# A decoder layer on one core: first loads and casts in halves, the last block of columns summed in two banks, stores from three queues

## The chip, the cores and the metric

The kernel runs on one core of one Trainium2 chip. A core has a matrix engine (PE, TensorE), a vector engine (DVE), a scalar engine (ACT), a small general engine (POOL, GpSimd) and an engine that here only starts transfers (SP). Each runs its own list of instructions strictly in order; they meet through semaphores. Transfers (DMA) are started from a queue of SP, ACT or POOL. The metric is the device time of one execution in microseconds (us), as a median over runs.

## What is computed

One layer of a hybrid decoder over 256 tokens of width 2048, all in float32. Two groups of heads share an input projection; a gated MLP follows, and a last normalisation. Cut to what matters here:

```
h    = rms_norm(x, attn_norm_g)
proj = h @ w_in                          # 2048 -> 4448 columns
y    = concat(rwkv7_mixer(...), mla_mixer(...))      # recurrent heads, attention heads
x    = x + y @ w_out
h    = rms_norm(x, ffn_norm_g)
x    = x + (silu(causal_conv3(h @ w_gate) + conv_b) * (h @ w_up)) @ w_down     # D_FF = 5632
return rms_norm(x, final_norm_g)
```

The reference works in float32. The kernel gets that accuracy from TensorE by splitting each operand in a rounded part "hi" and a rest "lo" and adding three products: hi·hi, hi·lo and lo·hi.

## The kernel before

**Weight pieces.** All weights stream once, in pieces of 128 x 1024 floats (512 KB). `piece()` (lines 125 to 135) starts the load on SP's queue (L127), lets ACT round the whole piece to hi (the cast of L133), and lets DVE form lo = raw − hi (L134). There are three buffers each for raw, hi and lo, so a load waits until the lo of the piece three before it is done.

**The input.** `xsplit(g)` (lines 137 to 146) loads four of the 16 row blocks of the transposed input (L139, one load of 512 KB). ACT scales each block by the norm's gain and rounds it (L143, four instructions of 256 columns). DVE forms the rest (L144). The gain lies in a small tensor `vec`, which ACT's own queue loads first (L122).

**The start.** The loop at lines 328 to 342 goes over g = 0 to 3: it loads input g, for even g also two weight pieces, one for each of two 128-row tiles of the projection, and multiplies (`prod_c`: for four row blocks first the eight products with hi, L175, then the four with lo, L178). SP's order there is the order of the code. The other engines' orders come from a scheduler that works when the program is built. After the loop come the sums of squares of x (`xt`), more tiles of the projection, and `rope_tables()`. In the last, DVE reduces angles (the `rp` tiles, L264 to L290), ACT takes sines (L292), and POOL copies the results to 32 blocks (`sinR`, `cosR`, L300 to L304). POOL also makes the shifted copies of `h` that the recurrent heads need (L383), behind those 32 blocks in its order.

**The MLP.** It goes in two blocks of 24 and 20 tiles of 256 columns of D_FF. Each block ends with the down projection: for each of four groups c of 512 output columns, `prod_a` (lines 188 to 197) accumulates both token blocks (tb 0 and 1, 128 tokens each) in one PSUM bank each, with three matmuls of 512 columns per row block of weights (L195, L196, L197). In the second block, at c = 3, the last four pieces of weights are already held in SBUF (the `wt` tiles). For these, token block 0 is summed to its end first, then token block 1, so that block 0 is finished while PE works on block 1.

**The end.** When a token block of c = 3 is summed, DVE adds it to the residual (L1008), ACT squares it and sums the squares of each token (L1013), and `final(tb)` runs: eight small DVE instructions for the reciprocal root (L216 to L225), the scaling of the four column groups (DVE L954 for c = 3 and L956 for c = 1, ACT L958 for c = 0 and 2), and four stores of 256 KB, all from SP's queue (L959). In the names of the profile the residual's tiles are all `x`.

Of the kernel before, what the change touches and what calls it, by code (L numbers as in the profile page):

```python
# [54 lines left out]
def hybrid_layer(ctx: ExitStack, tc: tile.TileContext, a: dict, out: bass.AP):  # L55
# [16 lines left out]
    def s4(dt=F32, n="s4"):  # L72
        return sb.tile([P, 1024], dt, tag="s4", name=nm(n), bufs=NS4)
# [20 lines left out]
    def mm(n="mm"):  # L94
        return ps.tile([P, 512], F32, tag="mm", name=nm(n), bufs=NMM)
# [38 lines left out]
        last_lo[0] = V.tensor_tensor(lo, raw, hi.bitcast(F32), ALU.subtract).ins  # L134
        return hi, lo

    def xsplit(g):
        raw = s4(n="xraw").rearrange("p (k t) -> p k t", k=4)
        nc.sync.dma_start(raw, xT[:, g * 4:(g + 1) * 4, :])  # L139
        for j in range(4):  # L140
            k = g * 4 + j
            h = xs_[g][:, j, 0, :]
            S.activation(h, raw[:, j, :], AF.Copy, scale=vv("ag", k))  # L143
            last_x[0] = V.scalar_tensor_tensor(xs_[g][:, j, 1, :], raw[:, j, :], vv("ag", k),  # L144
                                               h.bitcast(F32), ALU.mult, ALU.subtract).ins
        return raw
# [41 lines left out]
    def prod_a(accs, pieces, act_hi, act_lo, kt0, n, first, last, tbs=(0, 1)):  # L188
        hi, lo = pieces
        for j in range(n):  # L190
            wh, wl = hi[:, j * 512:(j + 1) * 512], lo[:, j * 512:(j + 1) * 512]
            for tb in tbs:
                ah = act_hi(kt0 + j)[:, tb * P:(tb + 1) * P]
                al = act_lo(kt0 + j)[:, tb * P:(tb + 1) * P]
                PE.matmul(accs[tb], ah, wh, start=first and j == 0, stop=False)  # L195
                PE.matmul(accs[tb], ah, wl, start=False, stop=False)  # L196
                PE.matmul(accs[tb], al, wh, start=False, stop=last and j == n - 1)  # L197
# [129 lines left out]

    with tc.manual_schedule(engines={mybir.EngineType.SP}):
        for g in range(4):
            xsplit(g)  # L330
            if g == 0:
                nc.scalar.dma_start(cst, a["cst"])
            if g % 2 == 0:
                for i in range(2):
                    pcs[i, g // 2] = piece(a["win"][wt0[i], g // 2])
            for i in range(2):
                hl = tuple(u[:, (g % 2) * 512:(g % 2 + 1) * 512] for u in pcs[i, g // 2])
                prod_c(acc0[i], hl, x_hl, g * 4, 4, g == 0, g == 3)
        for h in range(2):
            prod_c(acc0[2], piece(a["win"][26, h]), x_hl, h * 8, 8, h == 0, h == 1)  # L340
        sums(0)
        kacc[0] = in_tile(1)
        dve0 = last_lo[0]
        sums(1)
        kacc[1] = in_tile(2, ch)
        rope_tables()
        lora = s4(n="lora")
        nc.sync.dma_start(lora, a["lora"])
# [598 lines left out]
    def final(tb):  # L947
        part = st("part", 1)
        V.tensor_reduce(part, ssn[:, tb * 4:tb * 4 + 3], AX.X, ALU.add)
        rs3 = rsqrt(ssn[:, tb * 4 + 3:tb * 4 + 4], 1.0 / DM, EPS, 1, V, part)  # L950
        for c in (3, 0, 1, 2):
            xc = x1[c][:, tb, :]
            if c == 3:
                V.scalar_tensor_tensor(xc, xc, rs3, fgb[1][:, 512:1024], ALU.mult, ALU.mult)  # L954
            elif c == 1:
                V.tensor_scalar(xc, xc, rs3, None, ALU.mult)  # L956
            else:
                S.activation(xc, xc, AF.Copy, scale=rs3)  # L958
            nc.sync.dma_start(out[tb * P:(tb + 1) * P, c * 512:(c + 1) * 512], xc)  # L959

    f0 = 0
    for blk, nf in enumerate((24, 20)):
        hh = [s4(F32R, "hh").rearrange("p (k t) -> p k t", k=4) for _ in range(nf // 4)]
        hl = [s4(F32R, "hl").rearrange("p (k t) -> p k t", k=4) for _ in range(nf // 4)]
        for fi in range(nf):
            f = f0 + fi
            accs = []
            for gu in range(2):
                acc = mm()
                for h in range(2):  # L970
                    prod_b(acc, piece(a["wgu"][f, gu, h]), z_hl, h * 8, 8, h == 0, h == 1)
# [24 lines left out]
        for c in range(4):  # L996
            accs = [mm() for _ in range(2)]
            for i in range(n - (4 if blk == 1 and c == 3 else 0)):
                prod_a(accs, piece(a["wdn"][c, f0 // 2 + i]), h_hi, h_lo, i * 2, 2, i == 0, i == n - 1)
                if blk == 1 and i == 2:  # L1000
                    q = n - 4 + c
                    held.append((q, piece(a["wdn"][3, f0 // 2 + q], a8("wt"))))
            for tb in range(2):
                if blk == 1 and c == 3:
                    for i, pc in held:
                        prod_a(accs, pc, h_hi, h_lo, i * 2, 2, False, i == n - 1, (tb,))
                xc = x1[c][:, tb, :]
                V.tensor_tensor(xc, xc, accs[tb], ALU.add)  # L1008
                if blk == 0:
                    continue  # L1010
                o = tb * 4 + c
                scr = sb.tile([P, 512], F32, tag="xs", name=nm("scr"), bufs=2)
                S.activation(scr, xc, AF.Square, accum_out=ssn[:, o:o + 1])  # L1013
                if c < 3:
                    V.tensor_tensor(xc, xc, fgb[c // 2][:, (c % 2) * 512:(c % 2 + 1) * 512], ALU.mult)
                else:
                    final(tb)
        f0 += nf
# [81 lines left out]
```

## Time and profile before

| | us |
|---|---|
| median of 3 runs | 1210.38 (1208.66 to 1212.13) |
| the profiled execution | 1211.12 |
| its span on the core, first to last instruction | 1209.3 |
| PE busy in it | 1166.8 |
| DVE / ACT / POOL busy in it | 819.8 / 583.2 / 82.1 |
| mean granted TensorE clock | 0.985 of full speed |

The span is 1.8 us shorter than the execution's own time, which also counts what lies before and after it. Times inside the profile count from the start of the span. PE is busy through nearly all of it; what PE does not fill lies mostly in the first 50 us, in the recurrent and attention part between 250 and 420 us, and in the last 10 us.

### The profile page before, as it was taken

The numbers are of one execution on the slowest core, as the hardware profiler recorded it, in microseconds if no ns is written. First come the engines' busy times: TensorE is split into PE (matmuls) and PEld (weight loads), VectorE is DVE, ScalarE is ACT, GpSimd is POOL, SyncE is SP. The second block draws the span as 40 slices with busy tenths as digits, with TensorE's granted clock in tenths as the row PEclk, the third lists the DMA queues.
The fourth block names the chain that finished last, engine by engine and source line by source line (L and its number), as shares of the span: only waits on it lengthen the run. The fifth ranks groups of instructions, "written<-read, shape, count | busy, mean of one in ns | idle before, by whom it ended". The sixth has DMA issues, their size and how long they took to land.

```text
span 1209.3 us, 19618 instructions
## 1 busy us (share of the span) xinstructions
PE 1166.8 (96%) x7633; PEld 1029.2 (85%) x7633; DVE 819.8 (68%) x1304; ACT 583.2 (48%) x883; POOL 82.1 (7%) x248
## 2 busy tenths in 40 slices
PE   7899989988798999999999999999999999999996
PEld 7899989987686888888888888888888888888885
DVE  6797659766777556777777776444577777775563
ACT  6674335432334445655555554333455555554442
POOL 1500430301101001000000000000000000000000
PEclk9999999988899999999999999999999999999998
DMA  8555454734142555555555555556655555566672
GB/s 325 164 159 158 147 167 156 209 108 144 54 157 85 170 187 184 183 188 192 190 192 190 191 191 191 191 191 191 205 194 187 192 192 190 192 219 209 209 211 85
DMA packets 61486, 215.90 MB, mean 179 GB/s; under 512 B 7376, under 2 KB 8144, under 8 KB 61392
## 3 DMA queue, kind: packets, MB, share of 16 engines
q1 hardware_dynamic: 58544, 209.22, 52.8%
q0 software_dynamic: 2080, 3.38, 1.3%
q10 hardware_dynamic: 768, 2.05, 0.5%
q8 instruction: 60, 0.98, 0.3%
q14 instruction: 34, 0.28, 0.1%
HBM read 210.48 MB, written 3.41 MB: 177 GB/s over the span
## 4 chain that ended last, share of the span: by engine, by line
PE 87%; DVE 5%; POOL 2%; DMA 2%; ACT 2%; issue 1%; SPq 0%; ACTq 0%; DVEq 0%; POOLq 0%
PE mm L163 27%; PE mm L166 13%; PE mm L195 9%; PE mm L196 9%; PE mm L197 9%; PE mm L175 9%; PE mm L178 4%; PE pg L536 1%; DVE lo L134 1%; DMA T<-dU 1%; ACT hi L133 1%; DMA xraw<-in_xT 1%; PE py L687 1%; PE px L687 1%; POOL sinR L304 0%
## 5 line engine op out<-in xcount | busy, mean ns | idle before, releaser
L134 DVE TENSOR_TENSOR lo<-raw,hi 128x1024 fp32r<-128x1024 f32 x376 | 460.2, 1224 | 287.6 <-ACT hi L133 281.3
L133 ACT CAST hi<-raw 128x1024 fp32r<-128x1024 f32 x376 | 394.9, 1050 | 490.6 <-issue 223.6
L163 PE MATMUL mm<-z,hi 128*128 128x512 f32 x1408 | 351.3, 392 | 0.0
L163 PEld LDWEIGHTS mm<-z,hi 128*128 128x128 f32 x1408 | 251.9, 188 | 43.7
L166 PEld LDWEIGHTS mm<-z,lo 128*128 128x128 f32 x1408 | 188.3, 188 | 14.5
L166 PE MATMUL mm<-z,lo 128*128 128x256 f32 x1408 | 191.6, 278 | 0.0
L175 PE MATMUL mm<-x,hi 128*128 128x256 f32 x1056 | 147.8, 289 | 14.5 <-ACT hi L133 8.1
L175 PEld LDWEIGHTS mm<-x,hi 128*128 128x128 f32 x1056 | 135.4, 195 | 17.1 <-ACT hi L133 8.1
L196 PE MATMUL mm<-lo,hh 128*128 128x512 f32 x336 | 130.7, 389 | 0.0
L197 PE MATMUL mm<-hi,hl 128*128 128x512 f32 x336 | 130.7, 389 | 0.0
L195 PE MATMUL mm<-hi,hh 128*128 128x512 f32 x336 | 119.7, 389 | 0.0
L178 PE MATMUL mm<-x,lo 128*128 128x256 f32 x528 | 77.4, 286 | 0.0
L197 PEld LDWEIGHTS mm<-hi,hl 128*128 128x128 f32 x336 | 63.1, 188 | 13.2
L195 PEld LDWEIGHTS mm<-hi,hh 128*128 128x128 f32 x336 | 63.1, 188 | 13.0
L196 PEld LDWEIGHTS mm<-lo,hh 128*128 128x128 f32 x336 | 63.1, 188 | 13.0
L178 PEld LDWEIGHTS mm<-x,lo 128*128 128x128 f32 x528 | 69.6, 193 | 0.2
L196 PE MATMUL mm<-lo,yhi 128*128 128x512 f32 x128 | 51.5, 403 | 0.0
L197 PE MATMUL mm<-hi,ylo 128*128 128x512 f32 x128 | 50.5, 394 | 0.0
L195 PE MATMUL mm<-hi,yhi 128*128 128x512 f32 x128 | 49.7, 406 | 0.0
L974 POOL MEMSET gt<- 128x2 f32 x44 | 4.3, 99 | 575.9 <-DVE hl L986 559.0
L197 PEld LDWEIGHTS mm<-hi,ylo 128*128 128x128 f32 x128 | 24.2, 189 | 5.1
L196 PEld LDWEIGHTS mm<-lo,yhi 128*128 128x128 f32 x128 | 24.2, 189 | 5.0
(282 smaller groups left out, 1113.1 us busy)
## 6 DMA issues: line engine op xcount, KB each, us to landing
raw<-in_wgu SPq DMA_DIRECT2D x176, 512.0 KB, 3.3
raw<-in_wdn SPq DMA_DIRECT2D x88, 512.0 KB, 4.2
raw<-in_win SPq DMA_DIRECT2D x70, 512.0 KB, 3.6
raw<-in_wout SPq DMA_DIRECT2D x32, 512.0 KB, 3.6
raw<-in_wuq SPq DMA_DIRECT2D x6, 512.0 KB, 4.0
xraw<-in_xT SPq DMA_DIRECT2D x4, 512.0 KB, 6.3
xt<-in_x SPq DMA_DIRECT2D x4, 512.0 KB, 6.8
raw<-in_wuv SPq DMA_DIRECT2D x4, 512.0 KB, 3.8
```

The source lines that it names most:

```text
L133: S.copy(hi, raw)
L134: last_lo[0] = V.tensor_tensor(lo, raw, hi.bitcast(F32), ALU.subtract).ins
L163: PE.matmul(acc, hi[:, j * P:(j + 1) * P], act(kt0 + j), start=first and j == 0, stop=False, skip_group_check=True)
L166: PE.matmul(acc[:, :T], lo[:, j * P:(j + 1) * P], act(kt0 + j)[:, 0, :], start=False, stop=last and j == n - 1, skip_group_check=True)
L175: PE.matmul(acc, hi[:, j * P:(j + 1) * P], act(kt0 + j)[:, s, :], start=first and j == 0 and s == 0, stop=False, skip_group_check=True)
L178: PE.matmul(acc, lo[:, j * P:(j + 1) * P], act(kt0 + j)[:, 0, :], start=False, stop=last and j == n - 1, skip_group_check=True)
L195: PE.matmul(accs[tb], ah, wh, start=first and j == 0, stop=False)
L196: PE.matmul(accs[tb], ah, wl, start=False, stop=False)
L197: PE.matmul(accs[tb], al, wh, start=False, stop=last and j == n - 1)
L536: PE.matmul(pg[h][:, o:o + P], BK[pp][hs, gg, w * 2 + r, :, :], AR[pp][hs, gg, w * 2 + r, :, :], start=o == 0, stop=True, skip_group_check ...
L687: PE.matmul(dst[HS[h], a_ * 64:(a_ + 1) * 64], lhsT, rhs, start=n == 0 and a_ == 0, stop=True, skip_group_check=True)
L974: nc.gpsimd.memset(gt[:, 0:2], 0.0)
```

## The change

It has three parts.

1. `first_halves` replaces the first `xsplit(0)` and the first `piece()`. The first input load and the first weight load are each split in two of 256 KB, and they alternate: input, weights, input, weights. ACT casts the first weight piece in pieces of 256, 256 and 512 columns, with the input blocks in pairs in between; DVE does the same with lo.
2. At c = 3 of the second MLP block, token block 1 is summed in two banks of 256 columns (`mmh`, from the pool `ch`) by `prod_h`, with twice as many matmuls of half the width. With the held pieces one half is summed to its end, then the other. Each half has its own add and its own square; the two sums of squares (`sl`) are added by one more DVE instruction.
3. `final` issues its stores from SP (c = 3 and 0), POOL (c = 1) and ACT (c = 2).

```
-        raw = s4(n="xraw")...
-        nc.sync.dma_start(raw, xT[:, g * 4:(g + 1) * 4, :])
-        for j in range(4):
+    def first_halves(src):
...
+        for q in range(2):
+            cs = slice(q * 512, q * 512 + 512)
+            nc.sync.dma_start(xr[:, q * 2:q * 2 + 2, :], xT[:, q * 2:q * 2 + 2, :])
+            nc.sync.dma_start(raw[:, cs], src[:, cs])
+        for q in range(2):
+            cs = slice(q * 256, q * 256 + 256)
+            S.copy(hi[:, cs], raw[:, cs])
+            V.tensor_tensor(lo[:, cs], raw[:, cs], hi[:, cs].bitcast(F32), ALU.subtract)
+            xsplit(0, xr, (q * 2, q * 2 + 1))
+        S.copy(hi[:, 512:], raw[:, 512:])
+        V.tensor_tensor(lo[:, 512:], raw[:, 512:], hi[:, 512:].bitcast(F32), ALU.subtract)
...
-            nc.sync.dma_start(out[tb * P:(tb + 1) * P, c * 512:(c + 1) * 512], xc)
+            eng = (nc.sync, nc.gpsimd, nc.scalar, nc.sync)[c]
+            eng.dma_start(out[tb * P:(tb + 1) * P, c * 512:(c + 1) * 512], xc)
+    def prod_h(acc, pc, q, h_hi, h_lo, kt0, first, last):
+        for j in range(2):
+            wh, wl = (u[:, j * 512 + q * 256:j * 512 + q * 256 + 256] for u in pc)
+            ah, al = (f(kt0 + j)[:, P:2 * P] for f in (h_hi, h_lo))
+            for k, (l, r) in enumerate(((ah, wh), (ah, wl), (al, wh))):
+                PE.matmul(acc[:, :256], l, r, ...)
...
+                prod_a(accs, pc, h_hi, h_lo, i * 2, 2, i == 0, i == n - 1, (0,) if fine else (0, 1))
+                if fine:
+                    for q in range(2):
+                        prod_h(accs[1][q], pc, q, h_hi, h_lo, i * 2, i == 0, False)
...
+                if fine and tb == 1:
+                    sl = st("sl", 2)
+                    for q in range(2):
+                        cs = slice(q * 256, q * 256 + 256)
+                        for i, pc in held:
+                            prod_h(accs[1][q], pc, q, h_hi, h_lo, i * 2, False, i == n - 1)
+                        V.tensor_tensor(xc[:, cs], xc[:, cs], accs[1][q][:, :256], ALU.add)
+                        S.activation(scr[:, cs], xc[:, cs], AF.Square, accum_out=sl[:, q:q + 1])
+                    V.tensor_tensor(ssn[:, 7:8], sl[:, 0:1], sl[:, 1:2], ALU.add)
+                    final(tb)
```

In the new file the lines move: L139 and L127 of the start become L145 and L146 for the halves and L159 and L127 for the rest, L143 becomes L163, L1008 and L1013 become L1049 and L1051 for the halves, L959 becomes L982.

How it moves instructions is seen at three places. The first is ACT at the start of the program, from its first work after the loads of `vec` and `cst`. Before:

```order
L143 ACTIVATE x_65<-xraw_86,vec 128x256 x4
L133 CAST hi_99<-raw_97 128x1024
L133 CAST hi_105<-raw_103 128x1024
L143 ACTIVATE x_66<-xraw_133,vec 128x256 x4
L143 ACTIVATE x_67<-xraw_167,vec 128x256 x4
```

After, `raw_87` and `hi_88` are the first weight piece, and `raw_109` is the second:

```order
L163 ACTIVATE x_65<-xraw_86,vec 128x256 x2
L149 CAST hi_88<-raw_87 128x256 x2
L163 ACTIVATE x_65<-xraw_86,vec 128x256 x2
L152 CAST hi_88<-raw_87 128x512
L133 CAST hi_111<-raw_109 128x1024
L163 ACTIVATE x_66<-xraw_139,vec 128x256 x4
```

The first cast of weights now stands behind two input blocks instead of four, and the piece's cast is three instructions instead of one.

The second place is DVE at the end of the angle reduction in `rope_tables()`, around the lo of a weight piece and the small constants (`om_mu` to `idb`). Before:

```order
L134 TENSOR_TENSOR lo_347<-raw_344,hi_346 128x1024
L361 TENSOR_SCALAR om_mu<-vec 128x27
L272 SCALAR_TENSOR_TENSOR rp_441<-rp_442,rp_441 128x64
L362 TENSOR_SCALAR nkk<-vec 128x8
...
L375 CAST idb<-cst 128x128
L288 TENSOR_TENSOR rp_441<-rp_441 128x64
L272 SCALAR_TENSOR_TENSOR rp_441<-rp_442,rp_441 128x64
L290 TENSOR_SCALAR rp_441<-rp_441 128x64
```

After:

```order
L134 TENSOR_TENSOR lo_353<-raw_350,hi_352 128x1024
L308 TENSOR_TENSOR rp_447<-rp_447 128x64
L383 TENSOR_SCALAR om_mu<-vec 128x27
L384 TENSOR_SCALAR nkk<-vec 128x8
...
L397 CAST idb<-cst 128x128
L292 SCALAR_TENSOR_TENSOR rp_447<-rp_448,rp_447 128x64
L310 TENSOR_SCALAR rp_447<-rp_447 128x64
```

One step of the angles (L272 before) has moved ahead of that lo, so that three of them follow it instead of four.

The third place is DVE at the end, from the finishing of token block 0 to the sum for token block 1. `x_4835` and `x_4841` are the residual of c = 3, `x_4625` and `x_4631` that of c = 1. Before:

```order
L220 SCALAR_TENSOR_TENSOR rt_11683<-ry_11682,rm_11681 128x1
L225 SCALAR_TENSOR_TENSOR ry_11682<-rt_11683,ry_11682 128x1
L954 SCALAR_TENSOR_TENSOR x_4835<-x_4835,ry_11682,fgb_10950 128x512
L956 TENSOR_SCALAR x_4625<-x_4625,ry_11682 128x512
L1008 TENSOR_TENSOR x_4835<-x_4835,mm_11538 128x512
L216 TENSOR_SCALAR rm_11730<-ssn_5337,part_11728 128x1
```

After:

```order
L240 SCALAR_TENSOR_TENSOR rt_11727<-ry_11726,rm_11725 128x1
L1049 TENSOR_TENSOR x_4841<-x_4841,mmh_11545 128x256
L245 SCALAR_TENSOR_TENSOR ry_11726<-rt_11727,ry_11726 128x1
...
L976 SCALAR_TENSOR_TENSOR x_4841<-x_4841,ry_11726,fgb_10956 128x512
L978 TENSOR_SCALAR x_4631<-x_4631,ry_11726 128x512
L1049 TENSOR_TENSOR x_4841<-x_4841,mmh_11546 128x256
L1052 TENSOR_TENSOR ssn_5343<-sl_11745 128x1
L236 TENSOR_SCALAR rm_11803<-ssn_5343,part_11801 128x1
```

The add of the first half now stands inside token block 0's reciprocal root; the add of the second half and the new sum of the two squares (L1052) stand where the one add stood.

More of the change, by code (lines that the diff above doesn't have):

```diff
@@ L135, in piece, with xsplit @@
         return hi, lo
-    def xsplit(g):
-        raw = s4(n="xraw").rearrange("p (k t) -> p k t", k=4)
-        nc.sync.dma_start(raw, xT[:, g * 4:(g + 1) * 4, :])
-        for j in range(4):
+    def first_halves(src):
+        xr = s4(n="xraw").rearrange("p (k t) -> p k t", k=4)
+        raw = sb.tile([P, 1024], F32, tag="raw", name=nm("raw"), bufs=NRAW)
+        hi = sb.tile([P, 1024], F32R, tag="hi", name=nm("hi"), bufs=NHI)
+        lo = sb.tile([P, 1024], F32R, tag="lo", name=nm("lo"), bufs=NLO)
+        for q in range(2):
[9 more added lines that the diff above has]
+        V.tensor_tensor(lo[:, 512:], raw[:, 512:], hi[:, 512:].bitcast(F32), ALU.subtract)
+        return hi, lo
+    def xsplit(g, raw=None, js=range(4)):
+        if raw is None:
+            raw = s4(n="xraw").rearrange("p (k t) -> p k t", k=4)
+            nc.sync.dma_start(raw, xT[:, g * 4:(g + 1) * 4, :])
+        for j in js:
             k = g * 4 + j
@@ L329, in hybrid_layer @@
         for g in range(4):
-            xsplit(g)
             if g == 0:
+                pcs[0, 0] = first_halves(a["win"][wt0[0], 0])
                 nc.scalar.dma_start(cst, a["cst"])
+            else:
+                xsplit(g)
             if g % 2 == 0:
-                for i in range(2):
+                for i in range(1 if g == 0 else 0, 2):
                     pcs[i, g // 2] = piece(a["win"][wt0[i], g // 2])
@@ L958, in final @@
                 S.activation(xc, xc, AF.Copy, scale=rs3)
-            nc.sync.dma_start(out[tb * P:(tb + 1) * P, c * 512:(c + 1) * 512], xc)
+            eng = (nc.sync, nc.gpsimd, nc.scalar, nc.sync)[c]
[5 more added lines that the diff above has]
+            for k, (l, r) in enumerate(((ah, wh), (ah, wl), (al, wh))):
+                PE.matmul(acc[:, :256], l, r, start=first and j == 0 and k == 0, stop=last and j == 1 and k == 2)
     f0 = 0
@@ L997, in hybrid_layer @@
             accs = [mm() for _ in range(2)]
+            fine = blk == 1 and c == 3
+            if fine:
+                accs[1] = [ch("mmh") for _ in range(2)]
             for i in range(n - (4 if blk == 1 and c == 3 else 0)):
-                prod_a(accs, piece(a["wdn"][c, f0 // 2 + i]), h_hi, h_lo, i * 2, 2, i == 0, i == n - 1)
+                pc = piece(a["wdn"][c, f0 // 2 + i])
+                prod_a(accs, pc, h_hi, h_lo, i * 2, 2, i == 0, i == n - 1, (0,) if fine else (0, 1))
+                if fine:
+                    for q in range(2):
+                        prod_h(accs[1][q], pc, q, h_hi, h_lo, i * 2, i == 0, False)
                 if blk == 1 and i == 2:
@@ L1003, in hybrid_layer @@
             for tb in range(2):
-                if blk == 1 and c == 3:
+                xc = x1[c][:, tb, :]
+                if fine and tb == 1:
[5 more added lines that the diff above has]
+                        V.tensor_tensor(xc[:, cs], xc[:, cs], accs[1][q][:, :256], ALU.add)
+                        scr = sb.tile([P, 512], F32, tag="xs", name=nm("scr"), bufs=2)
+                        S.activation(scr[:, cs], xc[:, cs], AF.Square, accum_out=sl[:, q:q + 1])
+                    V.tensor_tensor(ssn[:, 7:8], sl[:, 0:1], sl[:, 1:2], ALU.add)
+                    final(tb)
+                    continue
+                if fine:
                     for i, pc in held:
                         prod_a(accs, pc, h_hi, h_lo, i * 2, 2, False, i == n - 1, (tb,))
-                xc = x1[c][:, tb, :]
                 V.tensor_tensor(xc, xc, accs[tb], ALU.add)
```

## The prediction, made before the changed kernel had run

> **What bounds the kernel now.** I read the page first, then the timeline of the first 32 us, the chain of waits up to 46 us, the windows of the first 80 us, and last the timeline and the transfers of the final 10 us. The page:
>
> ```profile
> span 1209.3 us, 19618 instructions
> PE 1166.8 (96%) x7633; PEld 1029.2 (85%) x7633; DVE 819.8 (68%) x1304; ACT 583.2 (48%) x883; POOL 82.1 (7%) x248
> PE 87%; DVE 5%; POOL 2%; DMA 2%; ACT 2%; issue 1%; SPq 0%; ACTq 0%; DVEq 0%; POOLq 0%
> ```
>
> PE is busy for 96% of the span and makes up 87% of the chain that ended last. The change leaves PE's arithmetic alone, so all it can win lies in the first microseconds, where PE has no data, and in the last ten, where PE is done. The timeline of the start (start, us, engine, line, operation, in brackets the idle time before and its releaser):
>
> ```profile
> 5.28 1.71 ACT L143 ACTIVATE x<-xraw,vec 128x256 fp32r<-128x256 f32 x4 [2.61 <-DMA vec<-in_vec]
> 7.05 1.04 ACT L133 CAST hi<-raw 128x1024 fp32r<-128x1024 f32 x1
> 8.14 2.08 PE L175 MATMUL mm<-x,hi 128*128 128x256 f32 x8 [8.14 <-ACT hi L133]
> 8.40 1.05 ACT L133 CAST hi<-raw 128x1024 fp32r<-128x1024 f32 x1 [0.31 <-DMA raw<-in_win]
> 9.68 3.31 ACT L143 ACTIVATE x<-xraw,vec 128x256 fp32r<-128x256 f32 x8 [0.23 <-DMA xraw<-in_xT]
> ```
>
> PE starts at 8.14 because the first cast ends then. That cast waits in ACT's order for four input blocks, and these wait for `vec`, which lands at 5.28. The second cast waits for its load until 8.40, the next input blocks for theirs until 9.68. The chain of waits behind that, in order of time:
>
> ```profile
> 2.11 7.55 DMA xraw<-in_xT
> ...
> 15.60 5.41 DMA xt<-in_x
> ...
> 27.46 1.14 DVE lo L134
> ...
> 28.69 0.13 DVE rp L272
> ...
> 30.11 0.21 DVE rp L290
> ...
> 30.68 0.40 POOL sinR L304
> ...
> 45.21 0.23 POOL cosR L300
> ```
>
> PE is not on it. What counts is the transfers, then an lo of DVE, the angles behind it, and 15 us of POOL's copies. The windows of 8 us (busy time and count of PE, PEld, DVE, ACT, POOL; granted clock; share of the DMA engines; GB/s):
>
> ```profile
> 16.00:24.00 8.00, 8.00 (x71) 8.00 (x70) 6.75 (x20) 5.20 (x10) 0.00 (x0) 1.00 0.96 323
> 32.00:40.00 8.00, 6.71 (x58) 6.52 (x56) 6.16 (x13) 3.90 (x4) 7.36 (x13) 1.00 0.81 249
> 40.00:48.00 8.00, 6.24 (x40) 6.04 (x40) 4.66 (x11) 4.10 (x9) 7.06 (x25) 0.79 0.50 147
> 56.00:64.00 8.00, 8.00 (x64) 7.48 (x62) 8.00 (x21) 7.41 (x16) 0.20 (x2) 1.00 0.35 105
> ```
>
> The transfers are full at the start (0.96 in the first of these, 0.81 in the next). From 32 to 48 us PE has idle time and POOL has little; in the last window DVE has none. The longest idle time of PE there, from the timeline, and what held the work behind it:
>
> ```profile
> 41.76 3.17 PE L175 MATMUL mm<-x,hi 128*128 128x256 f32 x16 [3.05 <-DVE h L384]
> 45.88 0.48 DVE L387 SCALAR_TENSOR_TENSOR sh<-h,vec,sh 128x256 f32<-128x256 f32 x1 [3.15 <-POOL h L383]
> ```
>
> DVE waits 3.15 for POOL's copy of `h`, which stands behind `cosR` in POOL's order, and PE waits for DVE. So a lead that PE gains at 8 us is spent again at 32 to 48 us, unless POOL's copies start earlier too. The end:
>
> ```profile
> 1198.28 0.48 DVE L956 TENSOR_SCALAR x<-x,ry 128x512 f32<-128x512 f32 x1
> ...
> 1199.35 0.40 PE L197 MATMUL mm<-wt,hl 128*128 128x512 f32 x1
> 1199.79 0.69 DVE L1008 TENSOR_TENSOR x<-x,mm 128x512 f32<-128x512 f32 x1 [1.03 <-PE mm L197]
> 1200.57 0.63 ACT L1013 ACTIVATE scr<-x 128x512 f32<-128x512 f32 x1 [1.62 <-DVE x L1008]
> 1201.32 0.21 DVE L216 TENSOR_SCALAR rm<-ssn,part 128x1 f32<-128x1 f32 x1 [0.85 <-ACT scr L1013]
> 1201.57 0.15 DVE L217 TENSOR_SCALAR ry<-rm 128x1 int32<-128x1 int32 x1
> 1201.76 0.22 DVE L220 SCALAR_TENSOR_TENSOR rt<-ry,rm 128x1 f32<-128x1 f32 x1
> ...
> 1203.11 1.33 ACT L958 ACTIVATE x<-x,ry 128x512 f32<-128x512 f32 x2 [1.82 <-DVE ry L225]
> ...
> 1203.78 0.48 DVE L956 TENSOR_SCALAR x<-x,ry 128x512 f32<-128x512 f32 x1
> 1203.85 1.79 SPq L959 DMA_DIRECT2D out<-x  x4
> ```
>
> Here every step waits for the one before: 9.55 us from PE's last end (1199.75) to the end of the span. Behind the four issues of SP (1203.85 to 1205.64) come the transfers; their share of the 16 engines in tenths, from 1203.5 to 1209.3 in slices of 0.145 us:
>
> ```profile
> DMA  0000000079899999999999999992000000000000
> ```
>
> **Part 1, the halves.** Added: two loads on SP, two more casts, two more lo on DVE. Removed: nothing. The same bytes are asked for in the same order. ACT still starts at 5.28, since `vec` lands then. Two input blocks take 0.86 (half of 1.71). For a cast of 256 columns the nearest row is ACT's square of 256 columns (a group: busy us, mean ns, idle before):
>
> ```profile
> L778 ACT ACTIVATE csq<-cr 128x256 f32<-128x256 f32 x6 | 2.5, 416 | 1.9 <-DVE cr L773 1.6 <-DVE cl L782 0.3
> ```
>
> At 0.416 the first cast ends at 6.56 and PE can start at about 6.6 instead of 8.14, a lead of 1.5. Two such casts, two more blocks and one cast of 512 (0.63 by the square of 512 above) bring ACT to 8.46, and the second piece is cast at 8.46 instead of 8.40. The next blocks still begin at 9.68, when their load is there. So on ACT, and on DVE behind it, nothing after 9.68 moves: both follow the transfers, and these are full. Only PE has a lead, and in the windows it finds idle time of 1.29 (8.00 − 6.71) and 1.76 (8.00 − 6.24) before 48 us, in which DVE and POOL hold it. What moves POOL is DVE's order: one step of the angles now stands ahead of the lo of 27.46, so that `sinR` can start earlier by 0.13 (row of 28.69). Halves may cost bandwidth, since rows of 2 KB per partition stand where rows of 4 KB stood; the late lo would follow by at most as much. I take **−0.1**. The lower end is −1.5, the lead kept whole; the upper +0.5, a sixth of the 3.2 us that 1 MB takes at the 323 GB/s of the window.
>
> **Part 2, two banks.** Token block 1 has ten pieces of six matmuls at c = 3, six pieces in the common loop and four held: 60 matmuls of 512 columns become 120 of 256. Pace and prices have rows elsewhere in the MLP (three of the chain near 563 us, 8 matmuls of 512 columns and twice 8 of 256; then a group):
>
> ```profile
> 563.19 1.83 PE mm L163 x8
> 565.02 0.94 PE mm L166 x8
> 567.79 0.91 PE mm L166 x8
> L184 DVE TENSOR_TENSOR gt<-mm,gt 128x256 f32<-128x256 f32 x44 | 18.4, 417 | 0.0
> ```
>
> One of 512 takes 1.83/8 = 0.2288, two of 256 take 0.2275 to 0.235, in the mean 0.2313: 60 x 0.0025 = **+0.15**, with ends −0.08 and +0.37. Behind PE's last matmul the add falls from 0.69 to 0.42 (**−0.27**) and the square from 0.63 to 0.42 (**−0.21**). The sum of the two halves is a new small step on DVE; the nearest row is L217 at 0.15, and with the gap to its next it costs 0.19 (1201.57 to the next small one at 1201.76): **+0.19**. The first half's add and square are hidden: PE ends that half 24 matmuls (four pieces of six) x 0.1156 = 2.8 us before its last one. The add stands inside token block 0's reciprocal root and delays it by 0.42; that block's last DVE instruction ended at 1198.76 before, so now at about 1199.2, still ahead of PE's end near 1199.9. If that cover went, the second add would wait, 1 us for 1 us. On ACT the second square stands behind block 0's scaling and its store (0.45 an issue, 1.79/4), which end at about 1199.9 too, ahead of the add's end at 1200.3. Part 2 in sum: −0.14.
>
> **Part 3, three queues.** SP issued its four within those 1.79. Now c = 2 is issued at 1204.44 (1203.11 + 1.33) instead of about 1205.2, and c = 1 at 1204.26 from POOL. But the slices show the engines at 0.9 from 1204.66 to 1207.5: the four stores of 1.05 MB are limited by their own transfer, and the last issue is covered by the data before it. An earlier last issue wins only the thin first slices (0.7, 0.9, 0.8): **−0.1**. Lower end −0.3, the same 2.9 us of data with ten tenths instead of nine. The upper end comes from POOL's own transfers (count, KB each, median us to landing):
>
> ```profile
> out<-x SPq DMA_DIRECT2D x4, 256.0 KB, 2.4
> Lp<-dL POOLq DMA_DIRECT2D x1, 512.0 KB, 3.6
> TT<-dT POOLq DMA_DIRECT2D x4, 128.0 KB, 5.9
> ```
>
> By the 3.6 of `Lp` POOL's store lands at 1204.26 + 3.6 = 1207.86, against 1207.56 for the last of before: +0.3. By the 5.9 of `TT`: 1210.16, +2.6. I take it to land with the others, since `Lp` is twice as large.
>
> On this the Trainium skill ("DMA: Bandwidth & Descriptors", section "Issuing engines are not separate DMA queues") says that transfers from the scalar, sync and gpsimd engines all end up on the same 16 DMA engines and that issuing from several saves only the sequencer's time. The tenths above agree: the engines are at 0.9 with one queue. By that page part 3 wins nothing beyond the issue.
>
> **Sum.** −0.1 + 0.15 − 0.27 − 0.21 + 0.19 − 0.1 = −0.34. The profiled execution took 1211.12, so it would take 1210.8; it lies 0.74 above the median of the runs, 1210.38, so I forecast **1210.0**.
>
> **Rivals.**
> - *The lead is kept.* PE is full from 16 to 32 us (71 matmuls in 8.00 us), so a lead of 1.5 can live that long; if POOL's copies then start earlier too, because DVE finds its lo earlier, it lasts to the end. Two facts speak for it: the raw buffers are freed by DVE's lo, and the first piece's lo is done earlier, so that a later load may be asked for earlier. Against it: the transfers are at 0.96. The first eight matmuls took 2.08, 0.26 each, where later ones take 0.1127 (8.00/71): an early start also has the slow stretch over earlier. Time: 1210.0 − 1.4 = 1208.6. The Trainium skill ("TensorE: Matmul & The Clock Gate", section "What's actually happening") has TensorE at half clock until it has been busy for some 3.4 us; the 0.26 against 0.1127 agrees with that, and by the page the cold stretch starts at 6.6 and is over 1.5 earlier.
> - *POOL's store lands last.* It is decided by the 3.3 us from 1204.26 to 1207.56: if POOL needs longer from the wait to the landing, the end moves 1 for 1. `Lp` gives +0.3 and `TT` +2.6; at a middle of 1.4 the sum is −0.34 + 0.1 + 1.4 = +1.2, or 1211.6, slower than before. The Trainium skill ("Advanced Engine Details and Errata", section "DGE: Hardware vs Software") gives about 1 us to the first byte for a transfer from GpSimd and 0.6 for one from sync or scalar. By that the price is an estimated 0.4, less than what its earlier issue gives back.
> - *The halves of the end come out dearer.* If two matmuls of 256 cost 0.235 and block 0 is late on ACT, part 2 is +0.1 instead of −0.14: 1210.3, as before.
>
> **How the numbers follow.** The forecast has a chance of 0.60 (with the third rival, which ends beside it), the kept lead 0.20, POOL's late store 0.15; 0.05 is left for a rearranged stretch before 80 us that moves more. The lowest sum is −1.5 − 0.08 − 0.27 − 0.21 + 0.19 − 0.3 = −2.2, so 1208.2; the highest +0.5 + 0.37 − 0.29 + 2.6 = +3.2, so 1213.6. The range leaves out the last tenth of each side's rare case: 1207.7 to 1212.4, with 0.5 below the lowest sum for the runs' own scatter. A measurement tells a change from none at about 0.3%, 3.6 us: faster is below 1206.7, slower above 1214.0. Neither the lowest nor the highest sum gets there, so faster keeps 0.10 and slower 0.06, out of the kept lead and the unknown rearrangement, and of POOL's store.
>
> **What would show it.** Part 1: the first matmul at 6.6 and the second group of input blocks still at 9.68; `sinR` at 30.5. If `sinR` starts before 29.5 the kept lead is right. Part 2: from PE's last end to L236 1.28 instead of 1.57 us; and the last matmul 0.15 later relative to the start of c = 3. Part 3: the tenths full to the same place, three queues in them, and POOL's store not the last. The prediction is wrong if PE idles less than before between 30 and 50 us, or if the span ends over 1.8 us behind the last store's data.

## The result, and the profile after

The changed kernel took 1214.57 us in the median of 20 runs (1211.36 to 1221.53); the kernel before took 1210.88 beside it. The ratio is 1.0034, with a 95% interval of 1.0021 to 1.0047: slower by 3.7 us, where 1210.0 was forecast and 1212.4 was the end of the range; it is also above the highest sum of the prediction, 1213.6. A few executions, one of them of 5572 us, were disturbed as a whole and do not enter the ratios, which are not simply the quotients of the medians. The profiled execution took 1212.15, with a span of 1210.4, and is one of the fastest of its kernel, so the trace shows only a part of the 3.7.

The timeline of the start after the change, ACT and PE:

```profile
5.10 0.91 ACT L163 ACTIVATE x<-xraw,vec 128x256 fp32r<-128x256 f32 x2 [2.41 <-DMA vec<-in_vec]
6.05 0.71 ACT L149 CAST hi<-raw 128x256 fp32r<-128x256 f32 x2
6.51 2.85 PE L195 MATMUL mm<-x,hi 128*128 128x256 f32 x8 [6.51 <-ACT hi L149]
7.28 0.91 ACT L163 ACTIVATE x<-xraw,vec 128x256 fp32r<-128x256 f32 x2 [0.51 <-DMA xraw<-in_xT]
9.19 1.05 ACT L133 CAST hi<-raw 128x1024 fp32r<-128x1024 f32 x1 [0.49 <-DMA raw<-in_win]
10.47 3.31 ACT L163 ACTIVATE x<-xraw,vec 128x256 fp32r<-128x256 f32 x8 [0.23 <-DMA xraw<-in_xT]
```

PE starts at 6.51, as forecast (6.6). But the second half of the input is there only at 7.28, the second weight piece at 9.19 instead of 8.40, and the next input blocks at 10.47 instead of 9.68. In this pair of profiles the transfers are 0.8 us later. The windows of 4 to 8 us, first of the kernel before, then of the changed one (share of the DMA engines and GB/s are the last two columns):

```profile
4.00:8.00 4.00, 0.00 (x0) 0.00 (x0) 1.68 (x4) 2.66 (x5) 2.46 (x5) 1.00 1.04 411
```

```profile
4.00:8.00 4.00, 1.38 (x5) 1.09 (x5) 1.79 (x5) 2.34 (x6) 2.40 (x5) 1.00 1.02 368
```

The engines are full in both (1.04 and 1.02), and with halves they move 368 GB/s instead of 411. POOL's first copy and PE's wait for `h` in the timeline after:

```profile
31.33 0.40 POOL L324 TENSOR_SCALAR sinR<-rp 32x64 f32<-32x64 f32 x1 [24.93 <-ACT rp L312]
...
42.48 3.46 PE L195 MATMUL mm<-x,hi 128*128 128x256 f32 x16 [3.45 <-DVE h L406]
```

POOL starts 0.65 later (30.68 before) and PE waits 3.45 instead of 3.05, for work that also comes later. One pair of profiles is not enough here: the section on the first loads compares all of them. The end:

```profile
1196.30 0.28 PE L990 MATMUL mmh<-wt,hl 128*128 128x256 f32 x1
...
1199.13 0.28 PE L990 MATMUL mmh<-wt,hl 128*128 128x256 f32 x1
1199.45 0.42 DVE L1049 TENSOR_TENSOR x<-x,mmh 128x256 f32<-128x256 f32 x1 [0.70 <-PE mmh L990]
1199.90 0.42 ACT L1051 ACTIVATE scr<-x 128x256 f32<-128x256 f32 x1 [0.97 <-DVE x L1049]
...
1200.44 0.16 DVE L1052 TENSOR_TENSOR ssn<-sl 128x1 f32<-128x1 f32 x1 [0.57 <-ACT scr L1051]
1200.64 0.21 DVE L236 TENSOR_SCALAR rm<-ssn,part 128x1 f32<-128x1 f32 x1
...
1203.16 0.81 SPq L982 DMA_DIRECT2D out<-x  x2
1203.78 0.35 ACTq L982 DMA_DIRECT2D out<-x  x1
1203.87 0.54 POOL L982 DMA_DIRECT2D out<-x  x1 [4.18 <-DVE x L978]
```

From PE's last end (1199.41) to L236 it takes 1.23 us instead of 1.57, and the stores are issued within 1.25 us instead of 1.79. Yet from PE's last end to the end of the span it takes 1210.4 − 1199.41 = 10.99 instead of 9.55. The share of the DMA engines in the last 8.0 us, in slices of 0.2 us, of the kernel before and of the changed one:

```profile
DMA  9993000000000000199999999999997000000000
```

```profile
DMA  0000000099999999999888000000000000000000
```

The last byte is moved 1.8 us ahead of the end before and 3.6 us ahead of it now: in those 3.6 us the slices show no transfer. POOL's store does land last of the four, since it is issued last and takes longest (count, KB each, median us from issue to landing; SP's four have 2.3):

```profile
out<-x ACTq DMA_DIRECT2D x2, 256.0 KB, 2.8
out<-x POOLq DMA_DIRECT2D x2, 256.0 KB, 3.5
```

Issued at 1203.87, it lands at about 1207.4, some 3.0 us ahead of the end. What SP waits for behind its last issue, in the changed kernel (us in total, times, longest), where before the wait for the stores was 2.2 and that for PE's queue 0.7:

```profile
SPq L1146 <- DMA out<-x: 3.3, 1, 3.3
SPq L1146 <- PEq L1146: 2.3, 2, 1.8
```

The second wait is put down to PE's queue, but PE had ended at 1199.41. Line 1146 is the last of the program, where the queues of all engines meet. Its instructions in POOL's and SP's queues (count, ns min/median/max, first and last start), first of the changed kernel, then of the one before:

```profile
L1146 POOLq EVENT_SEMAPHORE  x4: 17/17/17, 1209.6 to 1210.3; - x4
L1146 POOLq DRAIN  x3: 46/102/5747, 1203.8 to 1210.1; - x3
L1146 SPq DRAIN  x3: 7/7/7, 1207.9 to 1209.8; - x3
```

```profile
L1096 POOLq DRAIN  x3: 46/102/4452, 1062.4 to 1209.1; - x3
```

A DRAIN is an instruction of the queue itself. The first one of POOL starts with the store, at 1203.8, and lasts 5.75 us. SP reaches its own first DRAIN at 1207.9, some 0.5 us behind the last landing. POOL goes on only at 1209.6, when its DRAIN is over, and 0.8 us later the span ends. Before the change POOL's DRAIN took 4.45 us behind a last instruction of 0.10 us at 1062.39, and no one waited for it.

### The profile page after: what moved, and what is told of

It is laid out like the page before. It is cut to its first block, busy times and chain, and to the rows that moved or that the text cites. A ratio compares the mean times of both kernels' runs of the same rounds, so it can differ in the third digit from the quotient of the medians.

```text
span 1210.4 us, 19750 instructions
## 1 busy us (share of the span) xinstructions
PE 1167.0 (96%) x7693; PEld 1030.2 (85%) x7693; DVE 820.3 (68%) x1308; ACT 584.4 (48%) x887; POOL 84.0 (7%) x250
## 4 chain that ended last, share of the span: by engine, by line
PE 75%; issue 13%; DVE 5%; DMA 2%; POOL 2%; ACT 1%; SPq 0%; POOLq 0%; DVEq 0%; ACTq 0%
PE mm L183 25%; PE mm L186 13%; PE mm L195 9%; PE mm L215 6%; PE mm L216 6%; PE mm L217 6%; PE mm L198 4%; PE pg L558 1%; DVE lo L134 1%; DMA T<-dU 1%; DMA raw<-in_win 1%; DMA xraw<-in_xT 1%; ACT hi L133 1%; PE py L709 1%; POOL sinR L324 0%
## 5 line engine op out<-in xcount | busy, mean ns | idle before, releaser
L216 PE MATMUL mm<-lo,hh 128*128 128x512 f32 x324 | 126.1, 389 | 0.0
L217 PE MATMUL mm<-hi,hl 128*128 128x512 f32 x324 | 126.1, 389 | 0.0
L215 PE MATMUL mm<-hi,hh 128*128 128x512 f32 x324 | 115.7, 389 | 0.0
L216 PEld LDWEIGHTS mm<-lo,hh 128*128 128x128 f32 x324 | 60.8, 188 | 12.3
L216 PE MATMUL mm<-lo,yhi 128*128 128x512 f32 x128 | 52.1, 407 | 0.0
L216 PEld LDWEIGHTS mm<-lo,yhi 128*128 128x128 f32 x128 | 24.5, 192 | 5.1
```

## A measure that does not scatter

Runs of one kernel lie some 2 us to either side of their median. In the profiles what differs lies ahead of the MLP: its first matmul starts between 471.4 and 476.5 us, and from it to the first matmul of the first down projection it takes 266.06 us in all of them. From the first matmul of the first down projection to the end of the span, the profiles of kernels that are alike there agree within 0.2 us. Its first row, before and after:

```profile
739.45 0.39 PE L195 MATMUL mm<-hi,hh 128*128 128x512 f32 x1
```

```profile
738.26 0.39 PE L215 MATMUL mm<-hi,hh 128*128 128x512 f32 x1
```

This stretch takes 1209.3 − 739.45 = 469.85 us before and 1210.4 − 738.26 = 472.14 after: 2.29 of the 3.7 us lie in it. The expectations of the later runs call it the stretch from the "second down projection stage"; it is the first block's. In the table it is cut at PE's last end. "Median" is that of 11 or 12 runs, each with some 30 runs of before beside it.

| kernel | median, before beside it | ratio (95%) | to PE's last end | behind it |
|---|---|---|---|---|
| before | 1210.88 | | 460.30 | 9.55 |
| changed (20 runs) | 1214.57 | 1.0034 (1.0021 to 1.0047) | 461.15 | 10.99 |
| e1_halves | 1211.11, 1210.76 | 1.0006 (0.9994 to 1.0019) | 460.29 | 9.37 |
| e2_banks | 1211.63, 1210.76 | 1.0007 (0.999 to 1.0025) | 461.15 | 9.33 |
| e3_queues | 1212.76, 1210.76 | 1.0018 (1.0006 to 1.003) | 460.30 | 11.22 |
| e4_nopool | 1211.84, 1210.76 | 1.0004 (0.9991 to 1.0016) | 461.15 | 9.11 |
| e5_changed | 1213.89, 1211.06 | 1.0035 (1.0016 to 1.0054) | 461.15 | 10.96 |
| e6_banks_queues | 1212.49, 1211.06 | 1.0012 (0.9997 to 1.0028) | 461.15 | 10.95 |
| e7_pool_first | 1211.45, 1211.06 | 1.0006 (0.9993 to 1.002) | 461.14 | 9.14 |
| e8_banks_nopool | 1211.49, 1211.06 | 1.001 (0.9995 to 1.0026) | 461.15 | 9.23 |
| e9_late_banks | 1211.33, 1210.9 | 1.0 (0.9984 to 1.0015) | 460.45 | 9.16 |
| e10_casts | 1209.71, 1210.9 | 0.9983 (0.9964 to 1.0002) | | |
| e11_loads | 1211.68, 1210.9 | 0.9994 (0.9976 to 1.0012) | 460.30 | 9.37 |
| e12_all_loads | 1212.08, 1210.9 | 1.0006 (0.9992 to 1.002) | 460.30 | 9.43 |
| e13_pool_c3 | 1212.72, 1210.82 | 1.0025 (1.0008 to 1.0042) | 461.15 | 10.57 |
| e14_best | 1210.99, 1210.82 | 1.0006 (0.9992 to 1.0019) | 460.45 | 9.18 |
| e15_whole_loads | 1214.24, 1210.82 | 1.0029 (1.0015 to 1.0043) | 461.15 | 10.94 |

In the profile of e10 PE is only half as fast from about 10 us on (45 matmuls in the 10 us from 10 to 20, where in the kernel before 71 fit in 8 us), so only what lies ahead of that is used.

## The experiments

### Each part alone, and the change without a store from POOL

e1 has `first_halves` alone, e2 the two banks alone, e3 the three queues alone. e4 is the changed kernel with

```
-            eng = (nc.sync, nc.gpsimd, nc.scalar, nc.sync)[c]
+            eng = (nc.sync, nc.sync, nc.scalar, nc.sync)[c]
```

> The kernel before with part 1 alone (halves of the first loads and casts). Theory A, three separate costs: the loads in halves bring the second input load later (9.66 to 10.45 in the two profiles) and POOL's first copy later (30.68 to 31.33), so +0.7 us at 80 us, carried to the end: about 1211.6 against 1210.9. Theory B, the granted clock: the slower time comes from more windows of half clock between 240 and 400 us, whatever part shifts the start; then this part alone gives +2 to +4 us with a mean clock 0.002 to 0.004 lower than before. If neither holds, the time is that of before within 1 us.

> The kernel before with part 2 alone (two banks of 256 columns at the end). Nothing ahead of the last stage changes, so both theories agree on the start and the middle. Theory A: from PE's last end to the first small step of the reciprocal root 1.28 us instead of 1.57, PE +0.15: -0.1 to -0.3 us in all. Theory B: the same time as before and the same clock. A result 1 us or more above before would mean that the two banks cost something that the last profile does not show.

> The kernel before with part 3 alone (stores from SP, POOL and ACT). Theory A: the last data of the stores are written about 0.6 us earlier, but the span ends 3.6 us behind the last data instead of 1.7, since a store from POOL is waited for longer: +1.2 to +1.9 us, about 1212.4, with the mean clock of before. Theory B: the stores change the end by less than 0.5 us, the clock is that of before, and so is the time.

> The changed kernel with POOL's store moved to SP (stores of c = 3, 0, 1 from SP and c = 2 from ACT). Theory A: the 3.6 us between the last data and the end go back to about 1.7 and the time falls by 1.2 to 1.9 us against the changed kernel, to some 1213. Theory B: the time and the clock stay those of the changed kernel, about 1214.6 and 0.983.

The queues alone are slower by 1.0006 to 1.003, and 11.22 us lie behind PE's last end. The changed kernel without POOL's store has 9.11 there and is not to be told from before (1.0004). So theory A holds for POOL's store, with a time below the 1213 that it gave. The rows of e3, its last matmul, POOL's last issue and the DMA share in its last 8.0 us:

```profile
1202.48 0.40 PE L197 MATMUL mm<-wt,hl 128*128 128x512 f32 x1
...
1207.63 0.54 POOL L960 DMA_DIRECT2D out<-x  x1 [4.80 <-DVE x L956]
```

```profile
DMA  0000000069999999999999000000000000000000
```

Again 3.6 us of silence. Theory B fails on it: the price is there without any change at the start. The banks alone show what neither theory expected: PE's stretch is longer by 0.85 us (461.15 against 460.30), in every kernel that has them throughout c = 3, and never in one without. Halves alone gave 1.0006, at most 1.0019, with the mean clock of before (0.985): theory B's 2 to 4 us at a lower clock are not seen, and the 0.7 of A is neither shown nor excluded.

### The change again, parts left out, POOL's store made early

e6 is the changed kernel without `first_halves`, e8 the same without POOL's store. e7 lets POOL store for token block 0 only, 5 us earlier:

```
-            eng = (nc.sync, nc.gpsimd, nc.scalar, nc.sync)[c]
+            eng = (nc.sync, nc.gpsimd if tb == 0 else nc.sync, nc.scalar, nc.sync)[c]
```

> The changed kernel once more, beside the three below on one chip. Theory A (a store from POOL at the very end holds the end of the program by some 1.9 us, the rest of the change costs 1 us or less): 11.0 us from PE's last end to the end of the span, and 2 to 3 us over before, 1213 to 1214. Theory B (the 3.7 us are mostly the start in halves, through PE's wait for h and the clock): the same time, but the next kernel takes most of it away and the third none.

> The changed kernel without part 1 (two banks and three queues alone). Theory A: still 11.0 us from PE's last end to the end, and +1.5 to +2 us over before. Theory B: within 0.7 us of before.

> The changed kernel with POOL storing c = 1 of token block 0 only; block 1's stores go from SP (c = 3, 0, 1) and ACT (c = 2). Theory A, with the cost in the lateness of POOL's last store: 9.1 us from PE's last end to the end, as with no store from POOL at all, and within 1 us of before. A rival to that: POOL's queue costs its 1.9 us at the end of the program however early its store was; then 11.0 us again. Theory B: as the changed kernel.

> The kernel before with the two banks and with c = 2 stored from ACT, all else from SP; no halves at the start. Theory A: 9.1 us behind PE's last end instead of 9.55, so -0.4 us against before, which the runs can hardly tell from no change. Theory B agrees. Against the kernel with halves and the same end (which gave +0.5 us over before) it tells what the halves cost: A expects 0 to 1 us.

The result of the change is repeated (1.0035). With POOL's store for block 0 alone the end is that of a kernel without any (9.14 and 9.11), in the last 8.0 us of e7:

```profile
DMA  9997899500000000069999999999999100000000
```

So it is not a store from POOL's queue as such that costs, but one as late as this. The profile of e7 shows why. POOL's DRAIN is as long as in the changed kernel, 5.79 us, but it starts at 1199.9 with the earlier store and is over at 1205.7, while SP comes to its own only at 1208.6:

```profile
L1146 POOLq DRAIN  x3: 46/102/5786, 1199.9 to 1209.1; - x3
```

Without halves and with POOL's store (e6) the end has its 10.95. Its median lies 1.4 over before, close to the 1.5 to 2 that A expected, but so wide (0.9997 to 1.0028) that the runs alone would not show it; the 10.95 do. e8, which has no halves, came to 1.001, and e4, which differs from it by the halves, to 1.0004: this pair shows no cost of halves.

### Cheaper banks, and the first loads taken apart

e9 keeps 512 columns in the common loop and goes to halves for the four held pieces only, in two further banks; the first bank is added to the residual earlier. It has no store from POOL and no halves at the start. Against the changed kernel:

```
+                    V.tensor_tensor(xc, xc, accs[1], ALU.add)
+                    acch = [ch("mmh") for _ in range(2)]
...
-                            prod_h(accs[1][q], pc, q, h_hi, h_lo, i * 2, False, i == n - 1)
+                            prod_h(acch[q], pc, q, h_hi, h_lo, i * 2, i == held[0][0], i == n - 1)
```

e10 is before with the casts in parts and the loads whole, e11 the reverse. e12 has all ten loads of the start loop in two halves each:

```
+        for q in range(2):
+            nc.sync.dma_start(raw[:, q * 2:q * 2 + 2, :], xT[:, g * 4 + q * 2:g * 4 + q * 2 + 2, :])
```

> The kernel before with a cheaper form of part 2: token block 1 keeps 512 columns in the six pieces of the common loop; only the four held pieces go in halves of 256 to two further banks. c = 2 is stored from ACT, the rest from SP; no halves at the start. Theory A by the traces so far: PE from the first matmul of the second down projection stage on loses 0.85 us with two banks throughout, since all 120 matmuls of 256 columns run at 0.118 to 0.120 each; with 48 of them it loses 0.15 to 0.25, and the 9.1 to 9.2 us behind PE's last end stay: from that first matmul to the end 469.7 against 469.85 before and 472.1 in the changed kernel. In all -0.2 us, no change by the runs. Rival: the 0.85 us come from the change of width and not from the number, then 470.3.

> The kernel before with the first weight piece cast in 256, 256 and 512 columns and the first two loads whole. Theory C (the loads in halves are what delays the second input load): that load lands as before, the group of eight input scalings begins at 9.4 to 9.9, PE begins at 7.5 to 8.1; the same time as before within 0.5 us. Theory D (PE's lead itself is turned into a longer wait for h): 0.5 to 1 us over before.

> The kernel before with the first two loads in alternating halves and the casts whole. Theory C: the group of eight input scalings begins at 10.0 to 10.5 instead of 9.4 to 9.9, PE at about 8.1, and the time is 0.5 to 1 us over before. Theory D: no change beyond the runs' scatter.

> The kernel before with all ten loads of the start loop (four of input, six of weights) in two halves each, in the old order, casts whole. This takes the cost of halved loads five times: Theory C: the last input blocks and POOL's first copy are later by 2 us or more (sinR at 32.5 or later instead of 30.7), and the time is 1 to 3 us over before. Theory D, or no cost of halves at all: sinR within 0.5 us of before, and no change.

e9 came out as expected: 460.45 + 9.16 = 469.61. With 48 narrow matmuls instead of 120 PE's stretch is longer by 0.15 us instead of 0.85. That the sum lies 0.24 below before is not won by the halves: the store from ACT accounts for some 0.17 of it, and four kernels with all stores from SP and 512 columns have between 9.37 and 9.55 behind PE's last end.

The narrow matmuls' pace in the common loop of the changed kernel, from the first to the last of eight:

```profile
1175.26 0.28 PE L990 MATMUL mmh<-hi,hh 128*128 128x256 f32 x1
...
1176.10 0.28 PE L990 MATMUL mmh<-lo,hh 128*128 128x256 f32 x1
```

That is 0.84/7 = 0.120 us each, or 0.240 a pair. Where the 0.85 lie is read from the first matmul of c = 3 and the first of the held pieces, before and after:

```profile
1172.26 0.39 PE L195 MATMUL mm<-hi,hh 128*128 128x512 f32 x1
...
1188.58 0.40 PE L195 MATMUL mm<-wt,hh 128*128 128x512 f32 x1
```

```profile
1171.06 0.39 PE L215 MATMUL mm<-hi,hh 128*128 128x512 f32 x1
...
1187.99 0.40 PE L215 MATMUL mm<-wt,hh 128*128 128x512 f32 x1
```

From 739 us to c = 3 it takes 432.80 us in both. The common loop takes 16.93 us instead of 16.32, the held pieces up to PE's last end 11.42 instead of 11.17: +0.61 and +0.25. In the loop before, a wide matmul took 16.32/72 = 0.2267 us. After, by the start times of all rows, the 72 narrow ones take 8.59 us where 36 wide ones took 8.16, and the 36 wide ones of token block 0 between them take 8.34, or 0.2317 each. So the loop loses 0.42 on the narrow ones and 0.18 on the wide ones beside them. e9 leaves the loop at 16.32. Whether the number of narrow ones costs or the alternation with wide ones is not separated.

e10 and e11 take loads and casts apart, with one profile each. In e10, the casts in parts let PE start at 7.45 and the second group of input blocks begins at 9.50, in time (in e14, which opens in the same way, 7.89 and 9.88):

```profile
7.45 2.15 PE L193 MATMUL mm<-x,hi 128*128 128x256 f32 x8 [7.45 <-ACT hi L147]
...
9.50 1.71 ACT L161 ACTIVATE x<-xraw,vec 128x256 fp32r<-128x256 f32 x4 [0.23 <-DMA xraw<-in_xT]
```

In e11, the loads in halves alone bring that group at 10.21 although `vec` was there early, at 4.45. PE starts later than before, at 8.90:

```profile
4.45 0.91 ACT L159 ACTIVATE x<-xraw,vec 128x256 fp32r<-128x256 f32 x2 [1.77 <-DMA vec<-in_vec]
...
8.90 2.07 PE L191 MATMUL mm<-x,hi 128*128 128x256 f32 x8 [8.90 <-ACT hi L148]
...
10.21 0.91 ACT L159 ACTIVATE x<-xraw,vec 128x256 fp32r<-128x256 f32 x2 [0.24 <-DMA xraw<-in_xT]
```

In place this agrees with theory C, though PE was expected at 8.1. In size C expected too much. e12 has five times the halves; POOL starts at 32.00, between D's bound and C's. The times of e11 (0.9994, up to 1.0012) and e12 (1.0006, up to 1.002) neither show what C expected of them nor exclude it. The window of e12 from 4 to 8 us shows 365 GB/s, where the changed kernel has 368.

All profiles together say less than these pairs. The second group begins between 9.96 and 10.47 in the eight kernels with halves, and with whole first loads between 9.36 and 9.93 in eight and at 10.21 in e15. POOL's first copy starts between 30.39 and 31.33 in the seven kernels with halved first loads alone, and between 30.36 and 31.71 in eight with whole loads; the mean of both is 30.9. So the 0.65 us by which POOL starts later after the change is within what the profiles scatter.

### POOL's latency, the good parts together, the change with whole loads

e13 moves POOL's stores to c = 3, which DVE scales first; e15 is the changed kernel with its first two loads whole; e14 puts together e9 and e10.

```
-            eng = (nc.sync, nc.gpsimd, nc.scalar, nc.sync)[c]
+            eng = (nc.sync, nc.sync, nc.scalar, nc.gpsimd)[c]
```

> The changed kernel with POOL's stores moved to c = 3, which is scaled first, 0.67 us ahead of c = 1; c = 0 and 1 go from SP. If a store from POOL has a latency that counts from its issue, the end moves with it: 10.3 us from PE's last end to the end of the span instead of 11.0. If it is a fixed price at the end of the program, it stays 11.0.

> What came out well, together: the first weight piece cast in 256, 256 and 512 columns with whole loads; halves of 256 columns only for the four held pieces; c = 2 stored from ACT, all else from SP. Theory A: 469.6 us from the first matmul of the second down projection stage to the end (before 469.85), the second group of input scalings at 9.4 to 9.9. If the -1.8 us of the casts alone are real, about 1209 against 1211; if they were scatter, within 0.5 us of before.

> The changed kernel with its first two loads whole again and nothing else undone. If the halved loads cost 0.5 us or more at the start, the second group of input scalings begins at 9.4 to 9.9, and the time is 2.3 to 3 us over before instead of 3.7. If PE's lead itself is what costs, the time stays that of the changed kernel. In both cases 11.0 us behind PE's last end and 472.1 from the first matmul of the second down projection stage to the end.

POOL's last store in e13:

```profile
1204.89 0.54 POOL L982 DMA_DIRECT2D out<-x  x1 [4.18 <-DVE x L976]
```

Behind PE's last end (1200.83) that is 4.06 us, 0.40 earlier than in the changed kernel (4.46). The end came 0.42 earlier (10.57 against 10.99; the 10.3 expected had taken the time from one scaling to the next for 0.67, but they overlap). So the time counts from the issue. From the start of POOL's last issue to the end of the span it is 6.53 us in the changed kernel, 6.47 in e3, 6.51 in e5, 6.49 in e6, 6.51 in e13 and 6.49 in e15: the same 6.5 in all six. POOL's DRAIN lasts 5.71 to 5.75 us in them. From the end of SP's last issue to the end it was 3.7 us before (1205.64 to 1209.3).

e15 missed its expectation: its median lies 3.4 over before instead of 2.3 to 3 (1.0029; the interval, 1.8 to 5.2 us, covers this and the 3.7), and its second group of input blocks began at 10.21 in this profile, with whole loads, since `vec` itself came at 5.68. One profile can't show 0.5 us at the start. e14 is not faster than before (1.0006), so nothing is left of the 0.9983 of e10, which was probably scatter, and no kernel tried here is shown to beat the one before. In e14 the end has its 460.45 + 9.18 = 469.63, as in e9.

What the halved loads cost is left to the runs: the span of each run less the stretch behind 739 us of its kernel's profile. This rest is 740.2 us in the mean of 102 runs of the eight kernels that load in halves (changed, e1, e4, e5, e7, e11, e12, e13), 739.4 in 93 runs of the eight others that were changed, and 739.3 in 132 runs of before beside them. For e10 the stretch is taken as that of before. The difference is 0.8 us, with about 0.7 of uncertainty at 95% from the scatter of the runs. The kernels differ by more than that among themselves: their means lie between 739.2 and 741.0 with halves and between 737.6 and 740.2 without, and e4 and the changed kernel, whose starts are the same, lie at the two ends (739.2 and 741.0). Taken kernel by kernel the difference is 0.75, with 0.8 of uncertainty. So a cost of the halves is likely, but not firmly shown, and which wait it goes through stays open.

## Why the prediction was wrong, point by point

| term | forecast | measured |
|---|---|---|
| start in halves | −0.1 | +0.8, not firmly shown |
| PE with two banks | +0.15 | +0.85 |
| add, square and sum behind PE | −0.29 | −0.10 at the end (9.33 in e2, less 9.43, the mean of before, e1, e11 and e12) |
| stores from ACT | −0.1 with POOL's | −0.17 (9.16, mean of e4, e7, e8, e9, e14, less 9.33) |
| store from POOL | 0 | +1.8 (10.96, mean of the change, e5, e6, e15, less 9.16) |
| sum | −0.34 | +3.2 |

- **The step that failed first is the price of POOL's store, put at 0.** The prediction asked when POOL's bytes would land and compared that with the last landing of before. The bytes landed in time: 3.5 us from issue, close to the 3.6 taken from `Lp`, and the last of all was moved 0.4 us earlier than before, counted from PE's last end (7.4 against 7.8). But the end of the program did not wait for the bytes alone. It waited for POOL's queue, whose DRAIN of 5.71 to 5.75 us starts with the store, and followed POOL's issue by 6.5 us in six kernels: +1.8. The prediction had no term for that wait, but its own sign of being wrong, an end over 1.8 us behind the last data, shows it (3.6). The rival "POOL's store lands last" had the right sign, place and size (+0.3 to +2.6), and the store did land last of the four; but the late data that the rival prices did not occur, so its size is luck. The Trainium skill ("DMA: Bandwidth & Descriptors", section "Anatomy of one DMA — SWDGE (gpsimd) path") puts most of a fixed 2.0 us of such a transfer into the confirmation of the last byte, and by its fit 256 KB take an estimated 2.6 us. Here it was 3.5 to the landing, and 3.0 more to the end of the program, which is not in that fit.
- **PE's term was mis-sized.** The pair of narrow matmuls was priced at 0.2313, from a place where eight of 256 follow eight of 512. In the common loop a pair took 0.240, in the long row at the end 2 x 0.1179 = 0.236 (24 from 1196.30 to 1199.13). The wide one was taken at 0.2288, but in the loop before it took 0.2267. The prediction left the wide ones of token block 0 as they were; between narrow ones they took 0.2317, which is 0.18 of the 0.85. The upper end of the term, +0.37, was too low as well.
- **Behind PE the steps came as forecast.** In e2 L216 starts 1.29 us behind PE's last end (forecast 1.28, before 1.57). Of these 0.28 only 0.10 is left at the end of the span, where the kernels with the old end scatter by 0.18 (9.37 to 9.55).
- **The start was mis-sized, probably with the wrong sign.** That ACT waits for `vec`, that PE starts at 6.6 and that PE's lead is lost before 48 us came true. "The next blocks still begin at 9.68" did not. The prediction had seen that the transfers are full and that rows of 2 KB replace rows of 4 KB, and put the cost at the upper end (+0.5) instead of in the sum.
- **The kept lead** fell: what lies ahead of 739 us is no shorter with halves (740.2 against 739.4). The slow pace at the start is not over 1.5 us earlier either: the four matmuls at 9.16 still take 1.05 us, like the four at 10.02 before.
- **The cover of the last issue** was right: ACT's store alone wins 0.17.

The sum of the measured terms is +3.2 against +3.7 in the runs (2.5 to 5.7 by the interval). The 0.5 between is inside what the runs scatter; whether something of the change lies in it stays open. Why POOL's DRAIN takes 5.7 us behind a store, and 4.45 us behind the last instruction of before, stays open too: shown is that it starts with the issue, that the end waits for it, and that a store 5 us earlier costs nothing. Whether another instruction of POOL as late as this would hold the end in the same way was not run.

## What to carry to other kernels

A store is done when the program may end, not when its last byte is moved: measure the time between the last transfer and the end of the span, read what each queue does in it, and keep GpSimd's queue out of the last stores. When transfers are full, splitting them to start an engine sooner may be paid by what stands behind them (here a lead of 1.6 us won nothing), so look for what waits on the last byte, not the first. Price narrow matmuls in the order in which they will stand, with their neighbours. A stretch of the trace that repeats to 0.2 us settles what twelve runs with 2 us of scatter cannot.

## What the runs showed of the hardware that was not expected

- A store of 256 KB from POOL's queue held the end of the program for 6.5 us from its issue, within 0.06 us in six kernels, although it had landed after 3.5 us. What held it is a DRAIN of POOL's queue, 5.71 to 5.75 us long; with the store 5 us earlier (e7) the DRAIN took 5.79 us and was covered.
- In nine profiles without a store from POOL its DRAIN took 4.45 us, although it stands behind an instruction of 0.10 us.
- With the DMA engines full (share 0.99 to 1.04) the window of 4 to 8 us moved 364 to 388 GB/s in the eight profiles whose first loads have 2 KB per partition, against 404 to 411 in eight with 4 KB and 381 in a ninth (e15).
- Matmuls of 256 columns with a new weight block each took 0.114 to 0.1175 us beside the wide ones near 563 us, 0.118 in a long row at the end, and 0.120 in the common loop of the down projection. Wide ones (512 columns) took 0.2267 us in that loop alone, and 0.2317 between narrow ones.
